# One inference step on one core of a Trainium2: the written order of five instruction streams replaced up to the output of the first blocks of the MLP, and a test of transposed bits taken out

## The chip, the cores and the metric

The kernel runs on one core of one Trainium2 chip. The core has a matrix engine (PE, with its weight loads shown apart as PEld), a vector engine (DVE), a scalar engine (ACT), GpSimd (POOL) and a sync engine (SP), which here only issues DMA transfers. Each takes its own instruction stream in order, and waits on semaphores for the others. The metric is device time in microseconds (us): the median of several executions of the same program.

## The reference

One layer of a streaming encoder, on 1024 prompt rows and 64 sample rows of width 1024, in fp32:

```python
z = x @ w_in                                  # q,k,v of 6 "fox" heads, forget logits, u,v of the SGU, q,k,v of 6 "sb" heads
o_fox = softmax(q k^T / 8 + c_t - c_s) v      # causal; c = cumsum(log_sigmoid(f + b_f)); sample rows also see 512 cached rows
o_sgu = gelu(u) * (tril(w_s) @ layer_norm(gelu(v)) + b_s)      # within chunks of 128 rows
o_sb  = stick_breaking(q, k, v)               # sigmoid(z_ts) * prod_{s<j<t} (1 - sigmoid(z_tj)), strictly causal
x1 = layer_norm(ALPHA * x + rms_norm_heads([o_fox, o_sgu, o_sb]) * g_mix @ w_out)
y  = layer_norm(ALPHA * x1 + relu(x1 @ w_up)**2 @ w_down)       # w_up 1024 x 4096, w_down 4096 x 1024
```

The outputs are y, the new k and v rows of both attention groups, the log forget gates, and the normalised v rows of the SGU's open chunk.

## The kernel before, in words

An fp32 operand is held as two parts, the value rounded to the matrix engine's fast fp32 form ("hi", a copy on ACT or a cast on DVE) and the rest ("lo", the subtraction at L316 on DVE or POOL), and a product is three matmuls (hi hi, hi lo, lo hi; PASSES). So each weight and activation costs an ACT copy and a DVE or POOL subtraction before PE may use it.

The work runs in stages that overlap:

- Start and projections: loads of x and w_in, transposes of x on PE into xT0 (prompt half, lower columns of the contraction) and xT1, and the k and v projections of head pairs (L655, tiles kvfox2, kvfox1, kvfox0, kvsb0, kvsb1, kvsb2; "raw640_1", "row5", "row6" are pieces of w_in on their way to wkvfox2).
- Attention, pair by pair: scores S (L854), ACT exponent, the DVE scan and the POOL product for stick-breaking (L838, L840), transposes pt of the weights (L903), their hi and lo split (L870 on ACT, L316), the product o with v (L924 to L927), transposes of o back (L945). The SGU's products (sgv, sgm, sgu) are mixed in.
- Output projection mx (L522) with head norms (L449 to L480) and the first layer norm (L397 to L418), row block by row block, and the transposes of x1 into Strassen operands (L1500 to L1534, tiles xo, oTb).
- MLP up: z = x1 @ w_up in 16 blocks of 256 columns by a seven-product Strassen scheme in two row halves. Block p, half s has the accumulators zA, zB, zC, zD (L1626). ACT copies a finished zA to sn{p}_{s} (L1637), DVE adds the products into hh (L1640 to L1646), squares and clips (L1658), makes sums (L1667 to L1670), and SP stores them (h4_dr, h3_dr, hs_dr, L1671 to L1675). The weights of block p come as wr{p} (L1826), and are split into wa{p} (L1564, L316) and sums of blocks ws{p} (L1573 to L1577, L1857, L316). Blocks 0 and 1 borrow memory of the attention stage, the "rows": half 1 of block 0 keeps its hh in row6 (first four) and row5 (the others), and raws of block 1 lie in row0 and row2. From block 2 on buffers lie where the rows were, so that sn1_0 may be written only after the stores h4_dr<-row6 have left, and wr2, sn1_1 likewise after others (the guards at the end of the build).
- MLP down (L2103) from about 950 us on, with its accumulators, and the last layer norm.

What sets the order: the build notes every instruction in program order, and at its end a table ORDER holds for PE, ACT, DVE, POOL and SP a list of words. A word "n+k" takes n times the k-th of the instructions not yet placed. Each instruction then gets an order-only dependence on the one before it on its engine. So the table alone sets each engine's stream; the data waits follow from the tiles. A set "apart" held names that the table left out.

The test that the change removes stands in the attention's transposes (L904 to L914): for one block of pair fox1 and one of sb1 it transposes the same block a second time in plain fp32 (L907, tile same), subtracts the two on DVE (L909 to L911), sums the squares (L912), scales the sum by 2^80 and adds it to the constant negh (L913), which later norms use. It leaves negh as it is as long as the two transposes agree bit for bit.

## Time and profile before

| | |
|---|---|
| median of 3 runs | 1301.45 us (1300.45 to 1303.76) |
| time of the profiled execution | 1299.34 us |
| its span, granted clock of PE | 1297.6 us, 0.995 |
| busy in the span: PE, PEld, DVE, ACT, POOL | 98%, 91%, 75%, 56%, 46% |
| instructions: PE matmuls, DVE, ACT, POOL | 8853, 1812, 1560, 670 |

The profile is of one execution. Its span is 1.7 us shorter than its own time, and that time is 2.1 us under the median. "Busy" of PE is modelled, matmuls overlap, so that a pause shows as idle time only where it is longer than what is in flight. The views used below are: windows (busy time, granted clock and DMA share of a stretch), waits (idle time by the instruction that ended it), and the timeline (start, duration, engine, line, operation, number of like instructions in a row, and in brackets the idle time before it with what ended it).

### The profile page before, as it was taken

What the parts mean: (1) busy time and instruction counts of PE and PEld (TensorE: products, weight loads), DVE (VectorE), ACT (ScalarE), POOL (GpSimd) and SP (SyncE); (2) the same over time, 40 slices, a digit from 0 to 9 for tenths busy, and PEclk for the clock granted to TensorE, in tenths of its full rate; (3) what the DMA queues carried; (4) which work ended last, traced back from release to release, by engine and by line L of the source; (5) the groups of instructions that cost most, each with busy time, mean ns of one, the idle gap of its engine ahead of it and who ended that gap; (6) DMA issues with size and microseconds to landing.
All of it is one profiled execution on the core that took longest, in us unless ns stands there. A gap on an engine that the chain in (4) does not pass through costs nothing.

```text
span 1297.6 us, 24367 instructions
## 1 busy us (share of the span) xinstructions
PE 1268.3 (98%) x8853; PEld 1175.2 (91%) x8853; DVE 966.8 (75%) x1812; ACT 723.7 (56%) x1560; POOL 602.5 (46%) x670
## 2 busy tenths in 40 slices
PE   8999999999999999999899999999999999999996
PEld 8999999999989997778899999999988888888885
DVE  5678676778885687898678766766797667676777
ACT  4467676677675674344333222222367676676775
POOL 2232323257684666866122212121287656555567
PEclk9999999999999999999899999999999999999999
DMA  7445674322314376432324443535577443434433
GB/s 239 117 145 152 189 215 118 85 69 75 75 30 98 93 247 221 143 114 80 111 95 153 152 151 124 178 100 181 201 265 257 141 140 132 152 129 148 150 121 134
DMA packets 158049, 185.64 MB, mean 143 GB/s; under 512 B 27741, under 2 KB 116125, under 8 KB 157929
## 3 DMA queue, kind: packets, MB, share of 16 engines
q1 hardware_dynamic: 155832, 183.01, 44.5%
q8 instruction: 70, 1.15, 0.4%
q10 hardware_dynamic: 2096, 1.07, 0.3%
q14 instruction: 51, 0.41, 0.1%
HBM read 117.65 MB, written 60.10 MB: 137 GB/s over the span
## 4 chain that ended last, share of the span: by engine, by line
PE 79%; DVE 6%; POOL 5%; DMA 4%; issue 2%; ACT 2%; SPq 1%; DVEq 0%; POOLq 0%; ACTq 0%
PE A L2103 12%; PE zA L1626 11%; PE zD L1626 7%; PE D L2103 6%; PE kvsb L655 6%; PE kvfox L655 4%; PE zC L1626 4%; PE zB L1626 4%; PE B L2103 3%; PE Sfox L854 2%; PE mx L522 2%; PE qsb L795 2%; PE Ssb L854 2%; PE qfox L795 2%; PE sgu L655 1%
## 5 line engine op out<-in xcount | busy, mean ns | idle before, releaser
L316 POOL TENSOR_TENSOR wa<-wr,wa 128x512 fp32r<-128x512 f32 x41 | 56.6, 1403 | 233.1 <-ACT wa L1564 233.1
L316 POOL TENSOR_TENSOR wd<-rd,wd 128x512 fp32r<-128x512 f32 x77 | 104.0, 1361 | 109.2 <-ACT wd L1564 95.6
L1626 PE MATMUL zD<-xo,ws 128*128 128x288 f32 (+1 forms) x720 | 122.2, 287 | 0.1
L1626 PE MATMUL zA<-xo,ws 128*128 128x256 f32 (+1 forms) x720 | 113.1, 289 | 5.2 <-ACT sn L1637 5.2
L1626 PEld LDWEIGHTS zA<-xo,ws 128*128 128x128 f32 x720 | 99.5, 190 | 5.5 <-ACT sn L1637 5.5
L1626 PEld LDWEIGHTS zD<-xo,ws 128*128 128x128 f32 x720 | 102.9, 189 | 0.4 <-DVE hh L1640 0.4
L1637 ACT ACTIVATE sn<-zA 128x256 f32<-128x256 f32 (+1 forms) x80 | 30.8, 392 | 127.3 <-PE zA L1626 108.6
L522 PE MATMUL mx<-xT,oTb 128*128 128x512 f32 (+1 forms) x416 | 99.9, 394 | 1.0 <-DVE oTb L316 0.9
L655 PE MATMUL kvfox<-wkvfox,xT 128*128 128x256 f32 (+3 forms) x624 | 92.2, 289 | 2.5 <-DVE fx L758 1.3
L2103 PE MATMUL A<-wd,wd 128*128 128x512 f32 x312 | 94.2, 389 | 0.0
L522 PEld LDWEIGHTS mx<-xT,oTb 128*128 128x128 f32 (+1 forms) x416 | 75.6, 186 | 18.9 <-DVE oTb L316 1.7
L840 POOL TENSOR_TENSOR row<-row,row 128x127 f32<-128x127 f32 (+8 forms) x51 | 64.3, 1262 | 42.8 <-DVE row L838 34.2
L655 PEld LDWEIGHTS kvfox<-wkvfox,xT 128*128 128x128 f32 (+1 forms) x624 | 80.8, 187 | 3.1 <-DVE fx L758 1.5
L655 PE MATMUL kvsb<-wkvsb,xT 128*128 128x256 f32 (+1 forms) x624 | 79.7, 281 | 0.0
L1758 POOL TENSOR_TENSOR rd<-rd 128x512 f32<-128x512 f32 x56 | 73.3, 1310 | 10.1 <-DVE b L316 6.2
L2103 PE MATMUL A<-wd,h4a 128*128 128x512 f32 x240 | 77.7, 389 | 0.0
L838 DVE TENSOR_TENSOR_SCAN row<-row,one 128x128 f32<-128x128 f32 (+8 forms) x51 | 71.8, 1411 | 4.5 <-ACT row L837 3.4
L655 PEld LDWEIGHTS kvsb<-wkvsb,xT 128*128 128x128 f32 (+1 forms) x624 | 74.9, 186 | 0.0
L1564 ACT ACTIVATE wd<-rd 128x512 fp32r<-128x512 f32 x105 | 63.4, 621 | 17.3 <-POOL rd L1758 7.9
L2103 PEld LDWEIGHTS A<-wd,wd 128*128 128x128 f32 x312 | 58.6, 188 | 12.9
L2070 DVE TENSOR_TENSOR acc<-acc,A 128x512 f32<-128x512 f32 x73 | 49.6, 684 | 25.3 <-PE A L2103 24.8
L1626 PE MATMUL zB<-xo,wa 128*128 128x288 f32 (+1 forms) x360 | 66.5, 288 | 0.0
(729 smaller groups left out, 3861.6 us busy)
## 6 DMA issues: line engine op xcount, KB each, us to landing
h_dr<-hh SPq DMA_DIRECT2D x30, 512.0 KB, 3.2
rd<-w_down SPq DMA_DIRECT2D x30, 512.0 KB, 4.4
wr<-w_up SPq DMA_DIRECT2D x13, 1024.0 KB, 5.6
hr<-h_dr SPq DMA_DIRECT2D x31, 384.0 KB, 3.2
h_dr<-hh SPq DMA_DIRECT2D x30, 384.0 KB, 3.1
raw<-w_in SPq DMA_DIRECT2D x42, 256.0 KB, 3.2
wo_dr<-swo SPq DMA_DIRECT2D x32, 256.0 KB, 2.3
xT<-wo_dr SPq DMA_DIRECT2D x8, 1024.0 KB, 7.6
```

The lines of the kernel that those rows point to most:

```text
L316: eng.tensor_tensor(out, src, hi.bitcast(F32), op=ALU.subtract)
L522: nc.tensor.matmul(acc[0:m], oT[:, k, hx, 0:m], wo[k // 4][hw][:, k % 4, cs], start=(i == 0), stop=(i == len(seq) - 1))
L655: nc.tensor.matmul(acc[0:n, c0:c0 + n1 - n0], xT[k // 4][:, k % 4, c:c + n], wt[:, k, hw, n0:n1], start=(i == 0), stop=(i == len(seq) - 1))
L795: nc.tensor.matmul(acc[:, 0:w], wq[:, k, hw, :], xT[k // 4][:, k % 4, c:c + w], start=(i == 0), stop=(i == len(seq) - 1))
L838: nc.vector.tensor_tensor_scan(g[:, 0:n][:, ::-1], g[:, 0:n][:, ::-1], one.broadcast_to([P, n]), 1.0, op0=ALU.mult, op1=ALU.bypass)
L840: nc.gpsimd.tensor_tensor(s[:, 0:n - 1], s[:, 0:n - 1], g[:, 1:n], op=ALU.mult)
L854: nc.tensor.matmul(sps[:, b0 - c0:b0 - c0 + n], qd[:, h, s, half * P:(half + 1) * P], kp[b0 // 256][:, h, 0:n], start=(s == 0), stop=(s == ...
L1564: nc.scalar.activation(hi, raw, AF.Copy)
L1626: nc.tensor.matmul(z, w[:, hw, k], xop(s, bo, hx)[:, k, :], start=(new and k == 0 and j == 0), stop=(k == 3 and j == 2), skip_group_check= ...
L1758: eng.tensor_tensor(r[:, o], r[:, x], r[:, y], op=ALU.subtract)
L2070: nc.vector.tensor_tensor(out, out if other is None else other, bank, op=ALU.add)
L2103: nc.tensor.matmul(z, h[:, hx, q, o], wset[self.c % 2][q][:, hw, wb], start=((n in (0, 3) or n == 1 and self.c == 0) and q == 0 and j == 0 ...
```

## The change

All five lists of the table are replaced. The last 3363 instructions of PE (from zC of MLP block 4 on), 603 of ACT, 701 of DVE, 231 of POOL and 213 of SP stand in the same order as before, so the change reaches from the first load to about 690 us. No instruction is added. The test of the transposes' bits is gone, 2 PE and 10 DVE instructions, and with it the set "apart".

```diff
 ORDER["PE"] = """
-14 2+10 +12 1 +11 2+9 1 +8 1 +7 21 +14 2+10 +12 3+10 1 +9 +33 +36 1 2+32 +33 +32 2 2+6 +28 1 7+5 +51 1 +46 +19
...
+18 +10 3+6 2 +5 +4 1 2+3 19 4+8 2 +6 4 3+2 1 +25 1 7+24 7 3+47 4 +39 2 +11 2+36 +37 3 +15 2 +30 2+58 +54 1 +53 1 +54 1
...
@@ -901,17 +924,6 @@
                     for bi, (kb, half) in enumerate(blocks):
                         nc.tensor.transpose(ptr[:, bi * P:(bi + 1) * P], rows[half][1][:, kb * P:(kb + 1) * P], env["identr"])
-                    if nm in ("fox1_1_0", "sb1_1_0") and m == 1:
-                        at = len(traced)
-                        same = ps.tile([P, P], F32, name=f"same{nm}", tag="o", bufs=1)
-                        nc.tensor.transpose(same, rows[0][0][:, 2 * P:3 * P], ident)
-                        df = sa.tile([P, P + 1], F32, name=f"df{nm}", tag="df", bufs=1)
-                        nc.vector.tensor_copy(df[:, 0:P], same)
-                        nc.vector.tensor_tensor(df[:, 0:P], pt[:, 0:P], df[:, 0:P], op=ALU.subtract)
-                        nc.vector.tensor_tensor(df[:, 0:P], df[:, 0:P], df[:, 0:P], op=ALU.mult)
-                        nc.vector.tensor_reduce(df[:, P:P + 1], df[:, 0:P], axis=AX.X, op=ALU.add)
-                        nc.vector.scalar_tensor_tensor(negh, df[:, P:P + 1], 2.0 ** 80, negh, op0=ALU.mult, op1=ALU.add)
-                        apart.update(i.name for i in traced[at:])
                     n = len(blocks) * P
@@ -2470,7 +2482,7 @@
-        left = [i for i in traced[from_here:] if i.engine == e.engine and "Boundary" not in type(i).__name__ and i.name not in apart]
+        left = [i for i in traced[from_here:] if i.engine == e.engine and "Boundary" not in type(i).__name__]
```

What the lists do is seen in the streams that they give. In the changed file the lines behind the tables have numbers that are 23 higher up to the test and 12 higher behind it. Rows with x2 and more are like instructions in a row. Over the whole of PE's stream there are 4391 such rows before and 5238 after: the new order changes more often from one product to another. Three places follow.

**Start, DVE.** wkvfox2 is the weight of the first projection, xT0 and xT1 the transposed first row block of x. Before:

```order
L573 CAST m_sb_170<-m_sb_f_165 128x128
L626 CAST wkvfox2_214<-raw640_1_225 128x4x128
L316 TENSOR_TENSOR xT1_181<-xtp0_1_262,xT1_181 128x4x128
L316 TENSOR_TENSOR xT0_180<-xtp0_0_255,xT0_180 128x4x128
L316 TENSOR_TENSOR wkvfox2_214<-row6_116,wkvfox2_214 128x4x128
L316 TENSOR_TENSOR wkvfox2_214<-raw640_1_225,wkvfox2_214 128x4x128
L316 TENSOR_TENSOR wkvfox2_214<-row5_110,wkvfox2_214 128x4x128
```

Now:

```order
L596 CAST m_sb_170<-m_sb_f_165 128x128
L339 TENSOR_TENSOR xT1_181<-xtp0_1_262,xT1_181 128x4x128
L339 TENSOR_TENSOR xT0_180<-xtp0_0_255,xT0_180 128x4x128
L649 CAST wkvfox2_214<-raw640_1_225 128x4x128
L339 TENSOR_TENSOR wkvfox2_214<-raw640_0_221,wkvfox2_214 128x4x128
L339 TENSOR_TENSOR wkvfox2_214<-raw640_1_225,wkvfox2_214 128x4x128
L339 TENSOR_TENSOR wkvfox2_214<-row6_116,wkvfox2_214 128x4x128
```

The subtractions of xT1 and xT0, which wait for the transposes of x, now stand ahead of the cast of raw640_1. The first projection matmul reads that cast, in both orders. SP now asks for row6 ahead of raw640_0 and raw640_1, and the loads of the fox cache go from its first twenty places to places 55 to 86.

**Block 1 of the MLP, DVE and PE.** DVE before, from the last product of row6 that waits for zC to the last sum:

```order
L1644 TENSOR_TENSOR row6_116<-sn0_1_2_8931,zC0_1_9013 128x256
L316 TENSOR_TENSOR ws1_9010<-row2_92,ws1_9010 128x8x128
L1642 TENSOR_TENSOR row6_116<-zB0_1_8952,sn0_1_0_8929 128x256
L1646 TENSOR_TENSOR row5_110<-zD0_1_8979,sn0_1_1_8930 128x256
L1658 SCALAR_TENSOR_TENSOR row6_116<-row6_116 128x512
L1658 SCALAR_TENSOR_TENSOR row5_110<-row5_110 128x512
L1668 TENSOR_TENSOR h7_0_8798<-h7_0_8798 128x256
L1667 TENSOR_TENSOR row6_116<-row5_110 128x256
L1668 TENSOR_TENSOR row6_116<-row6_116 128x256
L1669 TENSOR_TENSOR h7_0_8798<-h7_0_8798 128x256
L1670 TENSOR_TENSOR row5_110<-row6_116,row5_110 128x256
L1669 TENSOR_TENSOR row5_110<-row6_116 128x256
```

Now, from the same instruction:

```order
L1656 TENSOR_TENSOR row6_116<-sn0_1_2_8915,zC0_1_8997 128x256
L1670 SCALAR_TENSOR_TENSOR row6_116<-row6_116 128x512
L1658 TENSOR_TENSOR row5_110<-zD0_1_8963,sn0_1_1_8914 128x256
L1670 SCALAR_TENSOR_TENSOR row5_110<-row5_110 128x512
L1679 TENSOR_TENSOR row6_116<-row5_110 128x256
L1680 TENSOR_TENSOR row6_116<-row6_116 128x256
L1681 TENSOR_TENSOR row5_110<-row6_116 128x256
L1682 TENSOR_TENSOR row5_110<-row6_116,row5_110 128x256
L1670 SCALAR_TENSOR_TENSOR h1_0_8783<-h1_0_8783 128x288
L1679 TENSOR_TENSOR h7_0_8782<-h1_0_8783,h7_0_8782 128x256
L1680 TENSOR_TENSOR h7_0_8782<-h7_0_8782 128x256
L1681 TENSOR_TENSOR h7_0_8782<-h7_0_8782 128x256
```

The subtraction ws1<-row2, and the sums of h7_0 (half 0 of block 0), went behind the chain on row6 and row5 that the two stores wait for. ws1<-row2 is now two rows below the last one shown. PE before, around its first product of zA1_0 with ws1, the one that may run only when ACT has copied the earlier zA1_0 to sn1_0:

```order
L1626 MATMUL zC0_1_9013<-xo13_8723,row1r_87 128x256 x4
L1626 MATMUL zD0_1_8979<-xo14_8722,oTb_7694 128x256
L1626 MATMUL zA1_1_9182<-xo14_8722,wa1_8922 128x256 x3
L1626 MATMUL zD0_1_8979<-xo14_8722,oTb_7694 128x256 x11
L1626 MATMUL zA1_1_9182<-xo14_8722,wa1_8922 128x256 x2
L1626 MATMUL zD1_0_9119<-xo0_7969,ws1_9010 128x288 x2
L1626 MATMUL zB1_0_9092<-xo0_7969,wa1_8922 128x288 x2
L1626 MATMUL zC1_0_9146<-xo0_7969,wa1_8922 128x288
L1626 MATMUL zA1_0_9076<-xo0_7969,ws1_9010 128x288
L1626 MATMUL zD1_0_9119<-xo0_7969,ws1_9010 128x288
```

Now, the last rows ahead of the same product:

```order
L1638 MATMUL zB1_0_9076<-xo0_7953,wa1_8906 128x288
L1638 MATMUL zA1_1_9166<-xo14_8706,wa1_8906 128x256
L1638 MATMUL zB1_0_9076<-xo0_7953,wa1_8906 128x288
L1638 MATMUL zD1_1_9215<-xo14_8706,ws1_8994 128x256
L1638 MATMUL zD1_0_9103<-xo0_7953,ws1_8994 128x288
L1638 MATMUL zC1_0_9130<-xo0_7953,wa1_8906 128x288
L1638 MATMUL zD1_1_9215<-xo14_8706,ws1_8994 128x256
L1638 MATMUL zD1_0_9103<-xo0_7953,ws1_8994 128x288 x2
L1638 MATMUL zA1_1_9166<-xo14_8706,wa1_8906 128x256
L1638 MATMUL zC1_0_9130<-xo0_7953,wa1_8906 128x288
L1638 MATMUL zA1_0_9060<-xo0_7953,ws1_8994 128x288
L1638 MATMUL zC1_0_9130<-xo0_7953,wa1_8906 128x288
```

Between the last zD0_1 and zA1_0<-ws1 there were seven matmuls; now there are 51. Nearly all of the others are products of block 1 (zA1_1, zB1_1, zC1_0, zC1_1, zD1_0, zD1_1) which stood behind it.

**The load of block 2's weights, ACT.** Before:

```order
L1857 ACTIVATE ws1_9010<-row0_80 128x8x128
L1857 ACTIVATE ws1_9010<-row2_92 128x8x128
L1637 ACTIVATE sn1_0_9074<-zA1_0_9076 128x288
L1826 DMA wr2_9090<-w_up 128x8x256
L1637 ACTIVATE sn1_0_9074<-zA1_0_9076 128x288
L1564 ACTIVATE wa2_9173<-wr2_9090 128x512 x2
L1637 ACTIVATE hh1_0_9075<-zA1_0_9076 128x288
```

Now:

```order
L1869 ACTIVATE ws1_8994<-row0_80 128x8x128
L1869 ACTIVATE ws1_8994<-row2_92 128x8x128
L1649 ACTIVATE sn1_0_9058<-zA1_0_9060 128x288
L1649 ACTIVATE sn1_1_9164<-zA1_1_9166 128x256
L1838 DMA wr2_9074<-w_up 128x8x256
L1649 ACTIVATE sn1_0_9058<-zA1_0_9060 128x288
L1649 ACTIVATE hh1_0_9059<-zA1_0_9060 128x288
```

The load wr2<-w_up, which ACT issues, has the copy sn1_1<-zA1_1 ahead of it now. That copy waits for the last of the zA1_1 products, which is the fourth row from the end of the PE rows above, and for the store of row5.

## The prediction

> **What bounds the kernel now.** I read the windows of the matrix engine (PE) first, since they say in which stages it waits at all. Columns: stretch, its length, PE's busy time and number of matmuls, granted clock, DMA share, GB/s.

> ```profile
> 0.00:475.00 475.00, 465.40 (x3962) 1.00 0.45 126
> 475.00:500.00 25.00, 22.74 (x176) 1.00 0.88 299
> 500.00:625.00 125.00, 123.11 (x667) 1.00 0.37 117
> 625.00:650.00 25.00, 19.75 (x141) 0.86 0.37 119
> 650.00:1275.00 625.00, 624.87 (x3862) 1.00 0.46 155
> 1275.00:1297.00 22.00, 12.40 (x55) 0.88 0.47 177
> ```

> From 650 us to the tail PE is idle for 0.13 us of 625. So that part is bound by PE's own work, and whatever PE saves before 650 us reaches the end, as long as the MLP's weights keep up. Before 650 us the idle time is 9.60 + 2.26 + 1.89 + 5.25 = 19.0 us, and one stretch has a lowered clock. The change touches just this part. Next the waits of PE, to see what that idle time is (total, times, longest):

> ```profile
> PE zA L1626 <- ACT sn L1637: 5.6, 2, 5.2
> PE warm L1402 <- POOL ident masks.py:199: 1.6, 1, 1.6
> PE kvfox L655 <- DVE fx L758: 1.3, 1, 1.3
> PE kvfox L655 <- ACT wkvfox L628: 1.2, 1, 1.2
> PE osb L924 <- ACT osbsb L937: 1.0, 1, 1.0
> PE Sfox L854 <- PE Sfox L854: 0.8, 1, 0.8
> PE osb L924 <- DVE dfsb L909: 0.4, 1, 0.4
> ```

> One wait stands out, and the rest is a few tenths here and there. Its timeline:

> ```profile
> 635.09 0.41 DVE L1646 TENSOR_TENSOR row<-zD,sn 128x256 f32<-128x256 f32 x1
> 635.42 1.28 DVE L1658 SCALAR_TENSOR_TENSOR row<-row 128x512 f32<-128x512 f32 x2
> 638.42 0.41 DVE L1669 TENSOR_TENSOR row<-row 128x256 f32<-128x256 f32 x1
> 637.86 0.32 SPq L1671 DMA_DIRECT2D h_dr<-row  x1
> 638.87 0.32 SPq L1672 DMA_DIRECT2D h_dr<-row  x1
> 640.62 0.41 ACT L1637 ACTIVATE sn<-zA 128x288 f32<-128x288 f32 x1 [7.82 <-DMA h_dr<-row]
> 635.54 0.29 PE L1626 MATMUL zC<-xo,wa 128*128 128x288 f32 x1
> 641.09 0.61 PE L1626 MATMUL zA<-xo,ws 128*128 128x288 f32 x1 [5.25 <-ACT sn L1637]
> 646.53 0.29 PE L1626 MATMUL zB<-xo,wa 128*128 128x256 f32 x1
> ```

> PE finishes half 1 of block 0, DVE runs the chain on row6 and row5 from 635.09 to 638.83, SP stores, ACT waits for the store before it may write sn1_0 over row6, and PE waits for ACT. What follows the wait costs as well:

> ```profile
> 641.00:644.00 3.00, 2.92 (x12) 0.50 0.96 258
> 644.00:647.00 3.00, 3.00 (x16) 0.58 1.07 360
> 647.00:650.00 3.00, 3.00 (x26) 1.00 0.25 62
> ```

> At half clock 12 matmuls go into 3 us. The 22 matmuls between 641.09 and 646.53 take 5.44 us; at the 26 in 3 us of the last row (0.115 each), or about 0.13 for the wider ones among them, they need 2.9. So the price of this one wait is 5.25 + 2.5 = 7.8 us. [...]

> **The change, part by part.** The sum is made against the profiled execution's 1299.34 us, which is 2.1 us under the median of 1301.45.

> *Block 1, -7.8 us.* On DVE, the chain on row5 starts when zD0_1 ends, as before, but loses what stood in it: after 635.09 come one clip (0.6), and two sums until h4_dr<-row6 may go (0.4 each), so about 636.9 in place of 637.86, and the second store about 637.8. On PE, 51 matmuls in place of seven stand between the last zD0_1 and the waiting product, 44 x 0.125 = 5.5 us more of work. The wait needs 5.25 us of cover and gets 5.5 + 0.9, so it ends about 1 us before PE is there. With no gap the clock stays up. If the store comes later than that, up to 1 us is free and the rest is a short gap without half clock; I bound the term between -5 and -7.8 (the hand-back, below, is a rival).

> *475 to 500 us, -2.0.* The window's idle time is 2.26 us, and its first wait is osb for ACT's copy of osb (1.0). That copy stood behind ACT's squares of the first output rows, which wait for POOL; now POOL's multiplications and ACT's copy come earlier. Between 0 and -2.3.

> *The first projection's fifth row block, -1.3.* kvfox waits for the DVE copy fx, which waits for ACT to write a buffer that two stores of k and v must have left. SP issued four loads of the fox cache ahead of these stores; they go forty places back and more. Between 0 and -1.3.

> *The test, -1.2.* Two transposes on PE, a wait of 0.4 for the test's DVE copy (dfsb), and the 0.8 of Sfox two microseconds behind the other test. Between -0.3 and -1.5.

> *Start, +0.7.* The first projection waits for the cast of raw640_1 on DVE, which now stands behind the two subtractions of xT:

> ```profile
> 6.19 0.43 DVE L626 CAST wkvfox<-raw 128x512 fp32r<-128x512 f32 x1 [3.42 <-DMA raw<-w_in]
> 6.78 1.29 DVE L316 TENSOR_TENSOR xT<-xtp,xT 128x512 fp32r<-128x512 f32 x2 [0.17 <-ACT xT L605]
> 7.78 1.92 PE L655 MATMUL kvfox<-wkvfox,xT 128*128 128x262 f32 x13 [1.21 <-ACT wkvfox L628]
> ```

> 6.78 + 1.29 + 0.43 = 8.5 in place of 7.78. Between 0 (the raw pieces also come in another order) and +1.

> *Finer mixing on PE, +5.* This is a cost that no idle time shows. A matmul of 128 columns among ones of 256:

> ```profile
> 106.52 0.35 PE L1004 MATMUL Ss0fox<-kc_fox,qsz 128*128 128x256 f32 x1
> 106.71 0.22 PE L903 MATMUL ptfox<-identr,row2r 128*128 128x128 f32 x1
> 106.77 0.33 PE L1004 MATMUL Ss0fox<-kc_fox,qsz 128*128 128x256 f32 x1
> 106.94 0.28 PE L924 MATMUL ofox<-pthfox,vpfox 128*128 128x256 f32 x1
> ...
> 204.55 0.33 PE L903 MATMUL ptfox<-identr,row4r 128*128 128x128 f32 x2
> 204.98 2.07 PE L655 MATMUL kvsb<-wkvsb,xT 128*128 128x256 f32 x16
> 206.88 0.28 PE L924 MATMUL ofox<-pthfox,vpfox 128*128 128x256 f32 x1
> ```

> A matmul of 256 columns takes 1.90 / 16 = 0.119 us from start to start. The single short one at 106.71 and its successor take 0.23 together, so the short one costs 0.11: its successor is held up. Five in a row from 204.55 to 204.98 cost 0.086 each. Along PE's order up to block 1 there are 1130 such short ones; 188 stood alone before and 410 do now, pairs go from 121 to 140, and runs of four and more, which held 487, hold 273. With 0.11 alone, 0.095 in pairs and threes, 0.086 in longer runs this is 20.7 + 43.2 + 41.9 = 105.8 us before and 45.1 + 42.6 + 23.5 = 111.2 now: +5.4, of which I take 5. Bounds: 0, if the gaps at which they now stand hide it, and +7, if changes between longer products cost too. [...]

> *The other gaps, -2.* Of the 9.60 + 1.89 us, 2.8 lie at the start, 1.3 and 1.2 are counted above; 6.2 are left in many small waits. Some lose their cause, others are made new by an order in which a consumer comes nearer to its producer. I take a third off, with bounds of -5 and +4.

> Sum: -7.8 - 2.0 - 1.3 - 1.2 + 0.7 + 5 - 2 = -8.6, so 1290.7 for an execution like the profiled one, and 1292.8 for the median.

> **The rivals.**

> *Mixing costs nothing.* Without the +5 the time is 1287.8. For it: short ones that fall beside a wait cost nothing. Against it: 98% busy leaves few waits.

> *Block 2's weights hand the gain back.* wr2 is loaded behind sn1_1 now:

> ```profile
> 640.78 0.39 ACTq L1826 DMA_DIRECT2D wr<-w_up  x1
> 648.16 1.16 ACT L1564 ACTIVATE wa<-wr 128x512 fp32r<-128x512 f32 x2 [1.01 <-DMA wr<-w_up]
> 655.70 0.29 PE L1626 MATMUL zA<-xo,wa 128*128 128x288 f32 x1
> ```

> Issue to copy takes 7.38 us while the DMA engines are full (0.96 and 1.07 above). The issue stays near 641.1, the copy's first half is done by 649.2, and PE, which used it at 655.70, now reaches its first use 73 matmuls behind zA1_0<-ws1, at 650.5. That is 1.3 us of room where there were over 5. If the load, its sums on DVE or the next block's load come 4 us late, the time is 1296.8.

> *DVE and POOL hold the attention and output stages.* DVE is full in one of them:

> ```profile
> 550.00:575.00 25.00, 24.87 (x43) 1.00 0.39 127
> ```

> Then the small gaps return elsewhere, and mixing costs its 7: -7.8 - 1.3 - 0.3 + 0.8 + 7 + 1 = -0.6, so 1301.

> *Slower.* In the same stage DVE adds the finished output products and so frees PE's accumulators. DVE has 0.13 us to spare there; where its new order makes it wait for a product that PE has put later, the whole wait goes on to PE, and a gap like that of block 1 costs 7.8. Two of them give 1308; it decides from 8.6 + 3.9 = 12.5 us of added waiting. Against it: the places on DVE there moved by few rows.

> **How the numbers follow.** My forecast of 1292.8 has a chance of 0.50 (its own range 1289 to 1297), mixing for nothing 0.20, the weights 0.10, DVE and POOL 0.11, slower 0.09. A difference of 0.3%, 3.9 us, is about what a measurement here can tell from no change: faster is below 1297.5, slower above 1305.4. Faster has 0.50 + 0.20 + half of the weights' case, 0.75; within it 0.16; slower 0.09. The range of 1285 to 1301 leaves out the best of the second case and all of the last.

> **What would show it.** In the profile after: PE's windows around 636 us without a gap over 1 us and a clock of 1.00; first projection at about 8.5; no 1.3 at fx; idle time before 475 us of about 7; and, for mixing, the same matmuls of 128 columns with PE's busy share unchanged though the stage ends earlier by less than the waits that left. I am wrong if PE waits for wa or ws after 650 us, if a new wait of over 2 us stands before 625 us, or if the end moves by the waits alone.

## The result, and the profile after

The change makes the kernel slower: 1315.26 us (1313.97 to 1318.7, four runs) against 1300.95 us (1298.16 to 1303.76, four runs), a ratio of 1.0114 with a 95% interval of 1.0084 to 1.0145. The forecast was 1292.8, and its range ended at 1301. The profiled execution of the change took 1313.97 us, 14.6 more than that of the kernel before.

The windows of PE in the changed kernel, with the columns of the forecast (stretch, length, busy time and matmuls, granted clock, DMA share, GB/s):

```profile
0.00:475.00 475.00, 460.32 (x3820) 1.00 0.42 118
475.00:500.00 25.00, 25.00 (x217) 1.00 0.68 222
500.00:625.00 125.00, 120.69 (x614) 0.99 0.44 142
625.00:650.00 25.00, 24.99 (x187) 1.00 0.32 106
650.00:1290.00 640.00, 639.61 (x3970) 1.00 0.46 156
```

Block 1 of the MLP, now near 660 us, has lost its wait: there is no idle time from 625 us on, and the clock is full. But the first 475 us hold 142 matmuls fewer than before (3820 against 3962), and their idle time has grown from 9.6 to 14.7. PE's waits (total, times, longest):

```profile
PE kvfox L678 <- ACT wkvfox L651: 2.3, 1, 2.3
PE ofox L938 <- DVE pthfox L339: 2.1, 1, 2.1
PE otpsb L957 <- ACT ptnnsb L893: 2.0, 1, 2.0
PE ptsb L926 <- DVE pthsb L339: 1.9, 2, 1.6
PE warm L1414 <- POOL ident masks.py:199: 1.6, 1, 1.6
PE kvfox L678 <- ACT kvsfox L779: 1.3, 1, 1.3
```

In place of one wait of 5.2 stand three of 2.0 to 2.3 and several of 1 to 1.6. Idle time, however, is not where the 14 us went: over the whole span it is 29.6 us now (1312.2 less 1282.6 busy) and was 29.3 (1297.6 less 1268.3). PE's busy time rose by 14.3 for the same products. One group of equal matmuls shows it, beside one that the change doesn't reach (busy us, mean ns). Before:

```profile
L522 PE MATMUL mx<-xT,oTb 128*128 128x512 f32 x400 | 98.1, 394 | 1.0 <-DVE oTb L316 0.9 <-DVE row3a L527 0.2
L2103 PE MATMUL A<-wd,wd 128*128 128x512 f32 x312 | 94.2, 389 | 0.0
```

Now:

```profile
L545 PE MATMUL mx<-xT,oTb 128*128 128x512 f32 x400 | 107.7, 405 | 0.4 <-DVE oTb L339 0.4
L2115 PE MATMUL A<-wd,wd 128*128 128x512 f32 x312 | 94.2, 389 | 0.0
```

The 400 products of the output projection are busy for 9.6 us more, though the time that they waited fell. Not all of that is lost time: the busy time of a group counts the stretches in which one of its products is under way, and it also grows where narrow ones part products that overlapped before. By their starts the loss there is about 5 us (see the account of the prediction). A place where narrow products now stand alone among them:

```profile
540.72 0.63 PE L545 MATMUL mx<-xT,oTb 128*128 128x512 f32 x2
541.19 0.22 PE L501 MATMUL op<-identm,row0br 128*128 128x128 f32 x1
541.25 0.68 PE L545 MATMUL mx<-xT,oTb 128*128 128x512 f32 x2
541.77 0.22 PE L501 MATMUL op<-identm,row0br 128*128 128x128 f32 x1
```

Two mx take 0.47 from start to start (540.72 to 541.19). The narrow one and the next two take 0.58 (541.19 to 541.77), so the narrow one costs 0.11, of which only 0.06 stand in its own interval; the rest is in the wide one behind it. Why that one is held up, nothing here shows.

To sum this up I took the time from each matmul's start to the next one's, up to the first zC product of MLP block 4, behind which PE's order is the same. From each interval the time that the shortest tenth of its width stays under in the kernel before is taken off (0.113 us for 256 columns, 0.224 for 512). What is left is put down as a wait where it is over 0.18 us, as half clock where the granted clock was 0.5, and else by its neighbours ("narrow" is up to 128 columns):

| us (matmuls) | before | change |
|---|---|---|
| waits over 0.18 | 28.3 | 28.4 |
| at half clock | 2.6 | 3.8 |
| narrow ones themselves | 55.4 (1107) | 49.1 (1096) |
| wide, right behind a narrow one | 32.4 (456) | 45.4 (653) |
| wide, ahead of a narrow one | 2.9 (333) | 5.7 (479) |
| wide among wide | 14.3 (3515) | 17.5 (3169) |
| the four lines of neighbours | 105.0 | 117.7 |

The neighbours give +12.7, half clock +1.2, waits +0.1: +14.0, and that zC product starts at 732.1 instead of 718.0 us. Of the waits before, 5.4 were block 1; so 5.5 us of other waits are new. Along equal amounts of PE's work the change is 8.2 us behind at 122 us of the order before, 11.2 at 350, 21.0 at 622, and then 13.8: block 1 gives back 7.3.

### The profile page after: what moved, and what is told of

It reads as the page before. It is cut to its first block, busy times and chain, and to the rows that moved or that the text cites. A ratio compares the mean times of both kernels' runs of the same rounds, so it can differ in the third digit from the quotient of the medians.

```text
span 1312.2 us, 24324 instructions
## 1 busy us (share of the span) xinstructions
PE 1282.6 (98%) x8851; PEld 1182.4 (90%) x8851; DVE 959.1 (73%) x1802; ACT 725.3 (55%) x1560; POOL 595.7 (45%) x670
## 3 DMA queue, kind: packets, MB, share of 16 engines
q10 hardware_dynamic: 2096, 1.07, 0.3%
## 4 chain that ended last, share of the span: by engine, by line
PE 89%; DVE 3%; DMA 3%; POOL 2%; ACT 2%; issue 1%; SPq 0%; DVEq 0%; ACTq 0%; POOLq 0%
PE A L2115 12%; PE zA L1638 11%; PE zD L1638 7%; PE mx L545 6%; PE D L2115 6%; PE kvsb L678 6%; PE kvfox L678 5%; PE zB L1638 4%; PE zC L1638 4%; PE B L2115 3%; PE qsb L818 2%; PE qfox L818 2%; PE Sfox L877 2%; PE Ssb L877 2%; PE sgu L678 2%; PE sgv L678 2%
## 5 line engine op out<-in xcount | busy, mean ns | idle before, releaser
L1638 PE MATMUL zD<-xo,ws 128*128 128x288 f32 (+1 forms) x720 | 126.7, 287 | 0.4 <-DVE hh L1652 0.3
L1638 PE MATMUL zA<-xo,ws 128*128 128x288 f32 (+1 forms) x720 | 116.2, 287 | 0.0
L678 PE MATMUL kvfox<-wkvfox,xT 128*128 128x256 f32 (+3 forms) x624 | 107.9, 297 | 3.6 <-ACT wkvfox L651 2.3
L545 PE MATMUL mx<-xT,oTb 128*128 128x512 f32 (+1 forms) x416 | 110.2, 405 | 0.4 <-DVE oTb L339 0.4
L678 PE MATMUL kvsb<-wkvsb,xT 128*128 128x256 f32 (+1 forms) x624 | 103.8, 290 | 0.1
L678 PEld LDWEIGHTS kvfox<-wkvfox,xT 128*128 128x128 f32 (+1 forms) x624 | 88.7, 191 | 4.4 <-ACT wkvfox L651 2.5
L545 PEld LDWEIGHTS mx<-xT,oTb 128*128 128x128 f32 (+1 forms) x416 | 72.4, 186 | 16.3 <-DVE oTb L339 0.8
L678 PEld LDWEIGHTS kvsb<-wkvsb,xT 128*128 128x128 f32 (+1 forms) x624 | 86.1, 187 | 0.7 <-DVE wkvsb L339 0.2
L863 POOL TENSOR_TENSOR row<-row,row 128x255 f32<-128x255 f32 (+8 forms) x51 | 62.6, 1231 | 51.6 <-DVE row L861 42.6
L1638 PE MATMUL zB<-xo,wa 128*128 128x288 f32 (+1 forms) x360 | 70.9, 287 | 0.0
```

Of the source, the lines that this page charges most:

```text
L545: nc.tensor.matmul(acc[0:m], oT[:, k, hx, 0:m], wo[k // 4][hw][:, k % 4, cs], start=(i == 0), stop=(i == len(seq) - 1))
L678: nc.tensor.matmul(acc[0:n, c0:c0 + n1 - n0], xT[k // 4][:, k % 4, c:c + n], wt[:, k, hw, n0:n1], start=(i == 0), stop=(i == len(seq) - 1))
L863: nc.gpsimd.tensor_tensor(s[:, 0:n - 1], s[:, 0:n - 1], g[:, 1:n], op=ALU.mult)
L1638: nc.tensor.matmul(z, w[:, hw, k], xop(s, bo, hx)[:, k, :], start=(new and k == 0 and j == 0), stop=(k == 3 and j == 2), skip_group_check= ...
```

## The experiments

The tables are numbers, so an edit is told by the rows that it moves (without line numbers, and without some digits of the tiles' names). Two orders are joined by what had started by a time T: each engine first does what it had started by T under the one, then the rest in the sequence of the other. Most instructions lie near the same place in both orders, so that such a joint should move little else; the loads of the fox cache are an exception.

**Block 1: the order before up to 615 us, then the change's.** DVE, first rows that differ from the kernel before:

```diff
+TENSOR_TENSOR row5b<-row5b,gb_7470 128x512
 TENSOR_TENSOR oTb<-xr,oTb 128x512
-TENSOR_TENSOR row5b<-row5b,gb_7470 128x512
...
+SCALAR_TENSOR_TENSOR h_0_8782<-h_0_8782 128x576
```

> All five lists of the order before up to what had started by 615 us, from there on the order of the change; the test is out. Against the kernel before, only block 0's end and block 1 of the MLP and the missing test are left of the change. Theory A (the change gains at block 1 what was forecast, and loses about 21 us ahead of it, by the two traces: the same amount of PE work is reached 21.0 us later at work 495 and 13.8 us later at work 510): the wait of 5.25 us and the half clock behind it leave, 1300.9 - 7.3 = 1293.6, with the test's 0.5 to 1.2 perhaps 1292.5. Rival B (the wait leaves only because PE arrives late and thin at block 1, so that with the earlier order in front of it the store of row6 is late again): 1299 to 1301. Rival C (block 2's weights then come late): a wait for wr2 or wa2 behind 650 us, 1297.

Measured: 1292.07 us, ratio 0.9937 (0.9914 to 0.9961). PE's windows in that run:

```profile
600.00:625.00 25.00, 24.63 (x167) 1.00 0.33 106
625.00:650.00 25.00, 25.00 (x204) 1.00 0.36 119
```

Theory A holds; no wait and no half clock at block 1, with PE on time. This kernel is faster than both. What the change does at block 1 is worth 0.9995 - 0.9937 = 0.0058, or 7.5 us (give or take 3.5), beside the run without the test (below); the whole rest of it costs 1.0114 - 0.9937, some 23 us (give or take 5).

**The same, with PE's old order through the waiting product.** Against the run above, PE only (first rows):

```diff
-MATMUL zA_0_8740<-xo_7953,oTb 128x288 x2
-MATMUL zD_0_8818<-xo_7953,oTb 128x288 x6
-MATMUL zB_0_8769<-xo_7953,row4r 128x288 x2
+MATMUL zA_0_8740<-xo_7953,oTb 128x288 x4
...
```

> The run with the order before up to 615 us and the change's behind it, but PE's list stays as before up to what had started by 648 us, the product that waited 5.25 us with it; DVE, ACT, POOL and SP follow the change from 615 us. Theory A (the wait left because of the 44 matmuls that PE has in front of it now; the shorter chain on DVE brings the store about 1 us forward): a wait of 4 to 4.5 us is left and the half clock behind it, ratio 0.998 to 0.999, about 1298. Rival B (the chain on DVE alone did it): wait under 2 us, ratio 0.994 to 0.995. If the store is not earlier at all: a wait of 5.3, ratio 0.9995.

Measured: 1299.74 us, ratio 1.0002 (0.9989 to 1.0014). A piece of its timeline, and PE's window behind it:

```profile
641.22 0.41 ACT L1619 ACTIVATE sn<-zA 128x288 f32<-128x288 f32 x1 [6.19 <-DMA h_dr<-row]
641.69 0.40 PE L1608 MATMUL zA<-xo,ws 128*128 128x288 f32 x1 [4.49 <-ACT sn L1619]
```

```profile
642.00:645.00 3.00, 3.00 (x14) 0.50 0.97 310
```

The wait is 4.49 instead of 5.25, and the half clock is back. So the other four engines' lists, with the shorter chain on DVE, are worth 0.8 us, and the matmuls that PE now has ahead of the product carry the rest. In the change itself the copy starts at 660.76 and PE comes to the product at 662.07:

```profile
660.76 0.41 ACT L1649 ACTIVATE sn<-zA 128x288 f32<-128x288 f32 x1 [6.09 <-DMA h_dr<-row]
662.07 0.29 PE L1638 MATMUL zA<-xo,ws 128*128 128x288 f32 x1
```

The copy is done at 661.17, 0.9 us ahead of PE.

**The test alone taken out.** All lists stay, and with them the set of names that they leave out.

```diff
-                    if nm in ("fox1_1_0", "sb1_1_0") and m == 1:
...
-                        nc.vector.scalar_tensor_tensor(negh, df[:, P:P + 1], 2.0 ** 80, negh, op0=ALU.mult, op1=ALU.add)
-                        apart.update(i.name for i in traced[at:])
```

> The kernel before with the test of the transposes' bits taken out (2 PE and 10 DVE instructions), every list as before. The forecast gave -1.2 us with bounds of -0.3 to -1.5: 1299.7. If the two waits at the test were covered elsewhere: 1300.9, no difference. If the order of the change around the test is what matters, nothing here tells it.

Measured: 1298.7 us, ratio 0.9995 (0.9983 to 1.0008): -0.7 us, between nothing and the forecast's -1.2, and not to be told from either.

**The start alone.** The change's lists up to 16 us, the order before behind them. On DVE:

```diff
-CAST wkvfox_214<-raw_1_225 128x4x128
 TENSOR_TENSOR xT_181<-xtp_1_262,xT_181 128x4x128
 TENSOR_TENSOR xT_180<-xtp_0_255,xT_180 128x4x128
+CAST wkvfox_214<-raw_1_225 128x4x128
```

> The kernel before (the test out) with all five lists as in the change up to what had started there by 16 us: the cast of raw640_1 on DVE behind the two subtractions of xT, row6 asked for ahead of raw640_0 and raw640_1. It tests the forecast's term of +0.7 (first projection at 8.5 in place of 7.78). By the trace of the change it starts at 9.49, with half clock behind it, and is 1.4 us behind after 15 us of PE work. Theory A (lost at the start is lost at the end): 1.0 to 2.5 us slower, ratio 1.0005 to 1.0015. Rival B (a later wait for loads takes it back): ratio 0.999 to 1.000.

Measured: 1298.48 us, ratio 1.0004 (0.9993 to 1.0014). The trace has the late start: a wait of 2.3 for wkvfox, the first projection at 9.55, half clock from 9.7 us (granted clock over the span 0.993, against 0.995 in the run without the test). Against the run without the test that is +0.0009, some 1.2 us, but the intervals overlap, so at the end it isn't shown.

**SP's list alone in the early part.** On the run with the order joined at 615 us, SP as in the change up to 100 us:

```diff
+DMA row_116<-w_in 128x4x128
 DMA raw_0_221<-w_in 128x4x128
 DMA raw_1_225<-w_in 128x4x128
-DMA row_116<-w_in 128x4x128
...
-DMA cache_fox_k_0_1004<-cache_fox_k 128x2x128
-DMA cache_fox_v_0_1006<-cache_fox_v 128x2x128
+DMA p_fox_k<-kvsfox_0_294 128x128
```

> The run with the order before up to 615 us and the change's behind it, with SP's list (the DMA issues alone) as in the change up to what it had issued by 100 us: row6 ahead of raw640_0 and raw640_1, and the loads of the fox cache some fifty places later, behind the stores that the first projection's copy fx waits for. It tests the forecast's term of -1.3. Theory A: the wait of kvfox for fx (2.0 us in that run, with half clock behind it, 1.3 before) leaves and nothing comes for it: 1.3 to 3 us less, ratio 0.991 to 0.9925. Rival B (the late cache loads make PE wait for kvsfox, 1.3 at 97 us in the change): fx goes, kvsfox comes, ratio 0.9935 to 0.9945.

Measured: 1293.34 us, ratio 0.9962 (0.9949 to 0.9974). PE's longest waits are these:

```profile
PE otpfox L929 <- ACT osbfox L921: 2.2, 2, 1.6
PE A L2087 <- DVE acc L2052: 2.1, 1, 2.1
PE warm L1386 <- POOL ident masks.py:199: 1.6, 1, 1.6
PE osb L908 <- ACT osbsb L921: 1.5, 1, 1.5
```

The wait for fx is gone, as the forecast said, and the end comes no earlier. Neither theory named what came in its place: not kvsfox, but the copies osbfox and osbsb, which ACT does, and a wait in MLP down. The profiled executions say where the gain went. PE reaches the first zC product of block 4 at 710.1 us, against 712.8 without SP's edit, so 2.7 us were gained up to there. Behind it, where the order is the same, it needs 583.4 us, against 579.7 to 581.6 in the other thirteen profiles, and 2.1 of that is the wait in MLP down. Whether SP's list or this one execution makes that wait was not tried.

**PE's narrow matmuls gathered in the change, first way.** PE's list only, up to 655 us.

```diff
-MATMUL kvfox_0_269<-wkvfox_214,xT_181 128x262 x2
-MATMUL xtp_1_309<-identr,row4r 128x128
-MATMUL kvfox_0_269<-wkvfox_214,xT_181 128x262 x2
+MATMUL kvfox_0_269<-wkvfox_214,xT_181 128x262 x4
 MATMUL kvfox_0_269<-wkvfox_214,xT_180 128x262 x2
-MATMUL xtp_1_309<-identr,row4r 128x128 x3
-MATMUL kvfox_0_269<-wkvfox_214,xT_180 128x262
-MATMUL xtp_0_351<-identr,row3r 128x128
...
+MATMUL xtp_1_309<-identr,row4r 128x128 x4
+MATMUL kvfox_0_269<-wkvfox_214,xT_180 128x262 x2
+MATMUL xtp_0_351<-identr,row3r 128x128 x4
```

> The change, with PE's list alone altered up to 655 us: matmuls of up to 128 columns are moved next to the next or last such group, past at most 8 wider ones, where nothing they need was still open in the trace; 658 groups become 311. All other lists and the work are the change's. Theory A (finer mixing is most of the loss: a matmul of 128 columns that stands alone costs 0.121 us with its successor's delay, one in a group 0.089, by the starts in the two traces): summed over the neighbours of every matmul, 13.0 us less, 1315.3 - 13 = 1302. Rival B (the loss is new waits on the other engines, and mixing fills time that would be idle): 1315, within 2. Rival C (moved matmuls come too late for ACT and DVE): slower than 1317.

Measured: 1312.25 us, ratio 1.0099 (1.0068 to 1.0129). Theory A gave 1302 and missed. By the sums of starts the neighbours cost 109.6 in place of 117.7, but waits rose to 35.0 and half clock to 7.3: +10.1 of waiting against -8.1. The largest new one:

```profile
PE xtp L619 <- DMA row<-x_sample: 2.6, 1, 2.6
```

PE now came to the transposes of x_sample before their load had landed.

**The same, with only moves that delay no reader.** The places are fewer:

```diff
 MATMUL xtp_1_412<-identr,row2r 128x128
-MATMUL kvfox_1_316<-wkvfox_214,xT_181 128x262 x3
 MATMUL pkfox_0_374<-ident,kvsfox_0_294 128x128
-MATMUL kvfox_1_316<-wkvfox_214,xT_181 128x262 x2
+MATMUL kvfox_1_316<-wkvfox_214,xT_181 128x262 x5
```

> The change, with PE's list alone altered up to 655 us, as in the run that gathered 658 groups of narrow matmuls to 311, but now only such moves are made as delay no matmul by more than the time that lay between its end and its reader's start in the trace of the change: 658 groups become 362. In the profile of the run with 311 groups the small delays of PE had shrunk by 8 us (117.7 to 109.6 with stretches at half clock left out) and the waits over 0.18 us and the half clock had grown by 10. Theory A (mixing is a real cost; the new waits of that run came from the moves): small delays 109 to 111, waits near 28, so the end is 6 to 9 us earlier than the change's 1.011 of the kernel before: ratio 1.004 to 1.007, about 1306. Rival B (PE's time comes back as waits whatever is saved, since DVE and ACT set the pace): ratio 1.010 to 1.012.

Measured: 1309.05 us, ratio 1.0075 (1.0058 to 1.0092). Neighbours 110.1, waits 27.3, half clock 4.0. The profiled execution took 1306.08, 7.9 less than the change's; the ratios differ by 0.0039, 5 us (give or take 4.5). Its projection:

```profile
L538 PE MATMUL mx<-xT,oTb 128*128 128x512 f32 x400 | 102.4, 398 | 0.0
```

405 ns are down to 398, against 394 before. Only PE's sequence differs, and waits did not grow: mixing costs by itself. The sum fell by 8.5 us; the move of the end, 5, is less, but its uncertainty takes in both.

**The opposite: narrow matmuls spread in the kernel before.**

```diff
-MATMUL xtp_0_454<-identr,row1r 128x128 x2
-MATMUL kvfox_1_316<-wkvfox_214,xT_181 128x262 x4
+MATMUL xtp_0_454<-identr,row1r 128x128
+MATMUL kvfox_1_316<-wkvfox_214,xT_181 128x262
+MATMUL xtp_0_454<-identr,row1r 128x128
+MATMUL kvfox_1_316<-wkvfox_214,xT_181 128x262 x3
```

> The kernel before (the test out), with PE's list alone altered up to 615 us in the opposite sense: in groups of narrow matmuls the next ready wide one is moved in between, where that delays no reader in the trace; wide matmuls that follow a narrow one go from 461 to 613 (659 in the change), and rows that differ from the row ahead only from 2567 to 2687 (3481 in the change). Theory A (each wide matmul behind a narrow one starts its successor 0.071 us later, and a narrow one then costs some 0.03 less, by the starts in the traces; PE-only gathering gave 7.6 us for 296 groups): 152 groups more cost 3.5 to 4.5 us, ratio 1.002 to 1.003 with the test's -0.0005 in it. Rival B (mixing costs nothing by itself): ratio 0.9995.

Measured: 1302.85 us, ratio 1.0031 (1.0020 to 1.0042), 4.7 us (give or take 2.2) behind the run without the test. Neighbours cost 109.0 instead of 105.0 (wide ones behind a narrow one: 604 in place of 456, 41.8 in place of 32.4), and waits were 26.6. Theory A holds: 152 more groups cost 0.026 us each in the sum and 0.031 at the end.

**Gathering in front of the order joined at 615 us**, first with 268 groups, then, by moves that delay no reader, with 318. PE, from the second:

```diff
 MATMUL xtp_0_454<-identr,row1r 128x128
+MATMUL kvfox_1_316<-wkvfox_214,xT_181 128x262 x6
+MATMUL kvfox_0_269<-wkvfox_214,xT_180 128x262 x2
 MATMUL kvfox_1_316<-wkvfox_214,xT_181 128x262
 MATMUL xtp_0_454<-identr,row1r 128x128 x2
-MATMUL kvfox_1_316<-wkvfox_214,xT_181 128x262 x4
-MATMUL xtp_1_412<-identr,row2r 128x128
```

> As the run with the order before up to 615 us and the change's behind it, and PE's list up to 615 us gathered in the same way: 453 groups become 268. Theory A: by the same sum 6.4 us less than that run, so 1287. Rival B (mixing costs nothing by itself): equal to that run within 2 us. Rival C (moves make waits): slower than it.

> The run with the order before up to 615 us and the change's behind it (1292.1, ratio 0.9937), with PE's list up to 615 us gathered under the same condition on its readers: 453 groups become 318. Theory A: 2 to 4 us less, ratio 0.991 to 0.992, about 1289. Rival B (DVE and ACT set the pace): ratio 0.9937, or above it if moved matmuls still come late, as in the run with 268 groups (0.9975).

Measured: 1297.11 us, ratio 0.9975 (0.9960 to 0.9990), and 1293.27 us, 0.9953 (0.9938 to 0.9968), against 0.9937 without gathering. Neighbours fell from 106.0 to 103.9 and 103.1, waits rose from 22.7 to 29.9 and 24.7. Here theory A missed twice: the first run is slower by its waits, the second gains nothing that can be measured. Where the order was already coarse, the time that PE's neighbours save comes back as waits, in these sums.

**The order joined at 122 and at 350 us.** On DVE, the first rows that differ from the kernel before in the second of the two:

```diff
-TENSOR_TENSOR Ssb_5_0_512_5537<-Ssb_5_0_512_5537,m_sb 128x128
 SCALAR_TENSOR_TENSOR g1v_5608<-g1v_5608,sgv_5547 128x256
 TENSOR_TENSOR pthsb_1_1_1_5493<-ptsb_1_1_1_5489,pthsb_1_1_1_5493 128x384
+TENSOR_SCALAR sgvv_5516<-sgvv_5516,sgst_5522 128x256
+TENSOR_TENSOR Ssb_5_0_512_5537<-Ssb_5_0_512_5537,m_sb 128x128
 TENSOR_TENSOR sgvv_5607<-g1v_5608,sgv_5547 128x256
-TENSOR_SCALAR sgvv_5516<-sgvv_5516,sgst_5522 128x256
```

> All five lists of the order before up to what had started by 122 us, the change's behind it; the test is out. By the two traces the change reaches the same amount of PE work 8.2 us later at that place, of which 4 us are three waits (first projection 2.4, kvfox1 at 97 us 1.4, ofox2 at 122 us 2.2, less those of before). Theory A (what is lost there stays lost): 8 us under the change, ratio 1.005, about 1307. Rival B (later stages wait for DVE or the loads anyway and take it back): ratio 1.009 to 1.011.

> All five lists of the order before up to what had started by 350 us, the change's behind it; the test is out. By the two traces the change reaches the same PE work 11.2 us later at that place, 8.2 at 122 us and 21.0 at the end of the attention and output stages. Theory A (the loss is spread over the stages, each keeping its own): 1.011 less 0.0085, ratio 1.002 to 1.004; with the runs that change the order at 122 (1.0074) and at 615 us (0.9937) that makes three points on one line of loss. Rival B (the loss lies ahead of 350 us in the main, and what is lost behind it follows from that): ratio 0.994 to 0.997.

Measured: 1308.66 us, ratio 1.0074 (1.0051 to 1.0097), and 1303.2 us, 1.0036 (1.0022 to 1.0050). With 1.0114 for the whole change and 0.9937 for the part behind 615 us, the order ahead of 122 us costs 5 us (give or take 5), that from 122 to 350 another 5 and that from 350 to 615 some 13 (each give or take 3.5). By the starts of the two traces it was 8.2, 3.0 and 9.8. The largest part is clear of noise and lies behind 350 us; both accounts spread the rest over the stages ahead, and nothing shows it taken back later.

**How a new wait arises.** The one of 2.1 us at 122 us in the change, in its timeline:

```profile
118.89 0.60 ACT L893 ACTIVATE pthfox<-ptfox 128x512 fp32r<-128x512 f32 x1 [0.45 <-PE ptfox L926]
121.45 0.29 DVE L850 CUSTOM_DVE_ANT_0 row<-Sfox,row 128x128 f32<-128x128 f32 x1 [3.32 <-DMA row<-c_dr]
121.67 1.28 DVE L339 TENSOR_TENSOR pthfox<-ptfox,pthfox 128x512 fp32r<-128x512 f32 x2
122.41 0.39 PE L938 MATMUL ofox<-pthfox,vpfox 128*128 128x256 f32 x1 [2.08 <-DVE pthfox L339]
```

ACT has the hi part at 119.49. The subtraction that PE needs stands on DVE behind a score operation that waits 3.32 us for the load of c_dr, the last of which SP had issued at 115.2. PE pays for another operation's transfer. No run isolated this wait. It was absent in the run that has the order before up to 122 us and in the one up to 350.

## Why the prediction was wrong, point by point

*Block 1, -7.8: right, in mechanism and, as far as the runs tell, in size.* -5.4 of waits and -2.6 of half clock by the sums, -7.5 (give or take 3.5) by the runs; the copy was ready 0.9 us ahead of PE, where about 1 was forecast; with PE's old order 4.49 us of the wait stay. The bound of -5 took it that a short gap passes without half clock, and the runs don't show that in general: in the change one of 2.04 us did, and behind one of 1.62 the clock was 0.50. The rival of block 2's weights did not happen: from 650 us on PE is idle for 0.39 us of 640.

*Finer mixing, +5 with bounds of 0 and +7: the right mechanism, and the largest part mis-sized, +12.7.* The spread run shows that the price taken was right where it was read: 0.026 a group, as 5.4 us for some 200 groups had implied. Two things were left out, and a third is what remains. Narrow ones among products of 512 columns went from 16 groups to 72; they cost 5.1 us more (wide ones behind them 1.2 to 5.4, ahead of them 0.4 to 1.7, themselves 1.6 to 4.8, less 73 more of them at 0.05), about 0.09 a group, and I had priced all by rows among 256 columns. Wide products among wide ones cost 3.2 more (14.3 to 17.5); changes between them were put into the upper bound and not into the value, and no run tells whether they are the cause. What remains, among narrower products, is +4.4, near the 5 that the forecast took for them. The section on the change had the count that should have warned: 4391 rows became 5238.

*Mixing costs nothing, the rival with 0 for that step.* The traces do not bear it out: a matmul of 128 columns costs 0.11 alone among mx products in the rows above, and 152 more groups of such narrow ones cost 4.7 us (give or take 2.2) in the spread run.

*The other gaps, -2 with bounds of -5 and +4; 475 to 500 us, -2.0; fx, -1.3; the test, -1.2; start, +0.7: together -5.8, and wrong in sign.* The waits named did leave, but the others grew from 22.9 to 28.4, +5.5, and half clock outside block 1 is 3.8 where there was none. The step that failed is the counting of each removed wait as a gain, with no price for the waits that come: fx leaves, and in the change 1.3 us for kvsfox comes, in the run with SP's list alone 1.6 for osbfox. The wait of 475 to 500 is gone and two, of 1.6 and 2.0, stand behind 504. The first projection came 1 us later than summed (9.49 for 8.5), and half clock followed. The sum left the subtractions of xT at their old time, 6.78, but they wait for ACT's copies of xT, which start at 6.61 in place of 5.69:

```profile
6.61 1.08 ACT L628 ACTIVATE xT<-xtp 128x512 fp32r<-128x512 f32 x2 [0.50 <-PE xtp L626]
7.72 1.29 DVE L339 TENSOR_TENSOR xT<-xtp,xT 128x512 fp32r<-128x512 f32 x2 [4.94 <-ACT xT L628]
8.73 0.63 ACT L651 ACTIVATE wkvfox<-row 128x512 fp32r<-128x512 f32 x1
8.93 0.42 DVE L649 CAST wkvfox<-raw 128x512 fp32r<-128x512 f32 x1
9.49 0.73 PE L678 MATMUL kvfox<-wkvfox,xT 128*128 128x262 f32 x2 [2.31 <-ACT wkvfox L651]
```

ACT's last copy for wkvfox and the cast on DVE end together, at 9.36 and 9.35. In the kernel before, too, the row of the forecast names ACT's copy as what PE waited for, and not the cast.

*The signs.* Of those that the forecast named for being wrong one came: new waits of over 2 us ahead of 625 us. And the idle time ahead of 475 us is 14.7 where it said about 7.

*The rivals.* The third, in which DVE holds the attention stages, mixing costs 7 and small gaps return, named both causes and got 1301, since it still took +1 for the gaps. The slower one had the sign with the wrong mechanism: no wait of 5 us arose at 550 to 575 us.

The difference of the forecast from the profiled execution, 23.2 us, is 7.7 of mixing, 11.3 of waits (5.5 and 5.8) and 3.8 of half clock, with 0.4 over.

## What to carry to other kernels

Where one engine is 98% busy, a new order has to be priced by what it does to that engine's stream as well as by its waits: count how often it changes between shapes, and price each kind of neighbour from its own rows. A wait that an order removes is gained only if the work behind it has nothing else to wait for. Here the small waits were forecast at -5.8 us and came to +5.5, while the one large wait, whose cause had been followed to its end, was gained in full; so take removed small waits as nothing until a run shows them. When a large change holds one good place, join the orders there: the part behind 615 us alone is 0.6% faster than the kernel before, the whole 1.1% slower.

## What the runs showed of the hardware

```profile
504.00:508.00 4.00, 2.38 (x22) 0.99 0.78 235
508.00:511.00 3.00, 3.00 (x16) 0.50 0.98 322
...
521.00:523.20 2.20, 0.16 (x2) 1.00 0.23 86
523.20:526.20 3.00, 3.00 (x17) 1.00 0.19 62
```

In the run joined at 350 us it followed a stretch in which PE was busy for 2.98 of 4 us, so that no gap in it was over 1.02:

```profile
407.00:411.00 4.00, 2.98 (x24) 0.97 0.51 121
411.00:414.00 3.00, 3.00 (x12) 0.50 0.00 0
```

By the traces' records of the clock, half clock ahead of the tail lasted 6.83 us once in the kernel before (639.72 to 646.55) and 3.41 us twice in the change (9.55 to 12.96 and 507.89 to 511.31). In the kernel before it stands behind the gap of 5.25 us, in the change behind gaps of 2.31 and 1.62. These two profiles say more when they are divided, ahead of the tail, into stretches of 3.41 us that begin and end with the records of the clock. At full clock, the two stretches in which PE was idle longest, 3.41 us in the kernel before (from 636.31) and 2.31 in the change (from 6.13), were followed by half clock; of the three with 1.60 to 1.86 us, all in the change, only the one with 1.62 was; of those with 1.25 or less none was. So in these two the idle time within one such stretch goes with the clock somewhat more closely than the length of a gap does (gaps of 2.04 and 2.08 us were not followed by half clock, that of 1.62 was). But it does not decide alone: 1.86 us passed at full clock, while in the run joined at 350 us 1.02 or less was followed by 0.50. What else decides is open.
